# Which engine copies the turned attention probabilities out of PSUM: two of three on VectorE and one on ScalarE, in place of one and two

## The chip, the cores and the metric

The kernel runs on one core of a Trainium2 chip. The metric is the time of one execution on the device in microseconds; less is better. Of the core's engines five are spoken of here: TensorE (PE in the profile, with its weight loads as PEld), VectorE (DVE), ScalarE (ACT), GpSimd (POOL) and SyncE (SP), which only issues transfers in this kernel.

## The reference, cut to what matters

Two transformer blocks over 256 tokens of width 1024, in float32. The first block has eight heads of dilated attention and eight heads of dense causal attention, and a dense feed-forward net. The second block has two layers: sixteen heads of compressed, selected and windowed attention (called NSA below), then sixteen heads of block attention (MoBA); each layer has a mixture of 32 experts and a gated embedding. At 256 tokens every one of these attentions is a softmax over at most 256 keys:

```python
logits = einsum('bqhd,bkhd->bhqk', qi, k) * scale      # plus a bias, or a mask
p = softmax(where(mask, logits, -inf), axis=-1)
out = einsum('bhqk,bkhd->bqhd', p, v)
```

The product with `v` contracts over keys, so the probabilities, which come out with queries on the partitions, must be turned to have keys on the partitions.

## The kernel before

All attention runs through `class Pair` (L612): two heads side by side. `scores()` (L618) has PE make the scores of both heads (eight matmuls, L622, tile `sps`); DVE adds the bias and takes the row maximum (L629, four instructions); ACT takes the exponential and the row sum (L631, four instructions); DVE takes the reciprocal of the sums (L633) and, in NSA, multiplies in a gate (L635); POOL scales the probabilities (L638, four instructions). `turn()` (L640) has PE transpose the three 128x128 blocks of each head into a PSUM bank (L645, tile `ptp`) and then copies 384 columns of the bank into SBUF as `PT` (L648): one copy a head, two a pair, put on ACT or DVE by a counter `nev` that runs over the whole kernel. `pv()` (L652) has PE multiply `PT` with the values (L654, L656, tile `ops`). In NSA four more matmuls follow every second pair (L1827). `Out.put` (L688) then takes the result of a head pair out of PSUM in two parts (ACT at L691, DVE at L692).

`attend()` (L664) sets the order: step i issues the scores of pair i, the turn of pair i-2 and the product of pair i-3. So a copy is used by PE one step after it is issued. There are 8 pairs in the first block, 16 in NSA and 8 in MoBA: 32 pairs, 64 copies.

The instructions of PE and SP run in the order of the program text, which is written by hand (`manual_schedule(engines={ENG.PE, ENG.SP})`, L265). The order of the others, DVE, ACT and POOL, is set by a planner when the program is built. P and PT come from one pool of five buffers (`sq2`, L270, `PB = 5`), PSUM banks from one pool of eight (`bank`, L267).

`stream()` (L435) puts other work between the steps of attention. In the first block and in NSA this is the rest of a projection and what hangs on it (`second()`, L1481 and L1884), and from some step on the first halves of the output projection (`OutProj.part`, L699; its matmuls are L541 to L543, and each weight tile is split into two parts by ACT, L536, and DVE, L537, or POOL). In NSA `second()` also normalises the second half of the queries: ACT squares (L603), DVE sums (L604), DVE works out the reciprocal root in small steps (L457 to L479), DVE scales one half of the tokens and POOL the other (L1571), and PE transposes the result (L730, tile `htp`) ahead of the scores of the pairs that need it.

After attention the arena that holds the weights gets room again and the transfers of the following stage run on.

Of the kernel before, what the change touches and what calls it, by code (L numbers as in the profile page):

```python
# [251 lines left out]
def block_kernel(ctx, tc, I, out):  # L252
    nc = tc.nc
    mm = nc.tensor.matmul
    V, A, G = nc.vector, nc.scalar, nc.gpsimd
# [11 lines left out]
    def bank(name="bank"):  # L267
        return psum.tile([128, 512], F32, tag="bank", name=name)

    def sq2(name="sq"):  # L270
        return pr.tile([128, 512], F32, tag="sq", name=name)
# [12 lines left out]
    def drop(*keys):  # L284
        for k in keys:
            arena.drop(k)
        W.pump()
# [318 lines left out]
    nev = [0]  # L606
# [5 lines left out]
    class Pair:  # L612
# [27 lines left out]
        def turn(self):  # L640
            self.pt = []
            for p in self.p:
                b = bank("ptp")
                for i in range(3):
                    nc.tensor.transpose(b[:, i * 128:(i + 1) * 128], p[:, i * 128:(i + 1) * 128], ident)  # L645
                pt = sq2("PT")
                nev[0] += 1
                (A.copy if nev[0] % 3 else V.tensor_copy)(pt[:, 0:384], b[:, 0:384])  # L648
                self.pt.append(pt)
            drop(f"P{id(self)}")  # L650

# [216 lines left out]
    def moe(l, router, rs):  # L868
# [195 lines left out]
        def overflow(T):  # L1064
# [4 lines left out]
            with tc.If(n > 0):  # L1069
                with tc.For_i(0, n, 1):  # L1070
# [44 lines left out]
                    for k in range(8):  # L1115
                        mm(b[:, 0:256], R.xe[:, k], gu[:, :, k * 128:(k + 1) * 128], start=k == 0, stop=k == 7)
                    hidden(R)
                    turn(R)
                    for c in range(2):
                        b = R.bank(f"y{c}")  # L1120
# [8 lines left out]
        for q in range(8):  # L1129
# [34 lines left out]
            for _ in range(0 if q else 3):  # L1164
                next(fill, None)
            turn(T)
            for _ in range(9 if q else 1):
                next(fill, None)
# [876 lines left out]
```

## Time and profile before

| | before |
|---|---|
| time, median of 3 runs | 880.39 us (879.73 to 885.22) |
| profiled execution, its own time | 883.1 us |
| its span, first to last instruction | 881.3 us |
| PE busy | 829.3 us (94%) |
| DVE busy | 512.2 us (58%) |
| ACT busy | 453.0 us (51%) |
| POOL busy | 225.0 us (26%) |
| mean clock granted to PE | 0.971 of full |

The profiled execution is one run, taken by itself; its time stands 0.3% above the median. A busy time is the time an engine spent in instructions. The ends of matmuls are modelled, so short waits of PE between matmuls do not show as idle time; they show on PEld or as a longer distance between starts. [...] Attention takes three stretches of the span: about 96 to 125 us, 401 to 473 us and 694 to 729 us.

### The profile page before, as it was taken

The numbers are of one execution on the slowest core, as the hardware profiler recorded it, in microseconds if no ns is written. First come the engines' busy times: TensorE is split into PE (matmuls) and PEld (weight loads), VectorE is DVE, ScalarE is ACT, GpSimd is POOL, SyncE is SP. The second block draws the span as 40 slices with busy tenths as digits, with TensorE's granted clock in tenths as the row PEclk, the third lists the DMA queues.
The fourth block names the chain that finished last, engine by engine and source line by source line (L and its number), as shares of the span: only waits on it lengthen the run. The fifth ranks groups of instructions, "written<-read, shape, count | busy, mean of one in ns | idle before, by whom it ended". The sixth has DMA issues, their size and how long they took to land. (4 is left out here: it accounts for less than half of the span.)

```text
span 881.3 us, 15729 instructions
## 1 busy us (share of the span) xinstructions
PE 829.3 (94%) x5660; PEld 647.4 (73%) x5660; DVE 512.2 (58%) x1479; ACT 453.0 (51%) x1106; POOL 225.0 (26%) x293
## 2 busy tenths in 40 slices
PE   8997999999999999999899999965899899999997
PEld 5995878999999988686667666635587778666656
DVE  5669656755454567678664544321688765543355
ACT  6675875544444456267675133420666774232463
POOL 2225542322222234214453200000122355000011
PEclk9998999999999999999799999995999899999999
DMA  9990429655556542446015699999463515799961
GB/s 307 385 375 31 146 81 399 237 191 171 198 179 188 182 144 96 161 141 237 1 50 197 254 378 406 408 397 379 157 207 129 208 66 193 293 384 406 408 262 49
DMA packets 85137, 200.05 MB, mean 227 GB/s; under 512 B 5776, under 2 KB 27584, under 8 KB 85056
## 3 DMA queue, kind: packets, MB, share of 16 engines
q1 hardware_dynamic: 82704, 195.61, 61.1%
q10 hardware_dynamic: 2352, 3.40, 1.1%
q8 instruction: 46, 0.75, 0.3%
q14 instruction: 35, 0.29, 0.1%
HBM read 197.93 MB, written 1.06 MB: 226 GB/s over the span
## 5 line engine op out<-in xcount | busy, mean ns | idle before, releaser
L537 DVE TENSOR_TENSOR s<-a,s 128x512 fp32r<-128x512 f32 (+3 forms) x281 | 189.5, 685 | 121.7 <-ACT s L536 87.0
L536 ACT CAST s<-a 128x512 fp32r<-128x512 f32 (+3 forms) x294 | 172.6, 600 | 169.8 <-PE pj L543 71.7
L541 PE MATMUL pj<-s,a 128*128 128x512 f32 (+3 forms) x456 | 176.1, 386 | 4.6 <-ACT a L518 3.0
L542 PE MATMUL pj<-s,a 128*128 128x512 f32 (+3 forms) x456 | 170.5, 374 | 5.9 <-DVE s L537 5.8
L543 PE MATMUL pj<-s,a 128*128 128x512 f32 (+3 forms) x456 | 170.4, 374 | 1.3 <-DVE a L519 1.2
L537 POOL TENSOR_TENSOR s<-a,s 128x512 fp32r<-128x512 f32 (+3 forms) x71 | 90.1, 1269 | 304.6 <-ACT s L536 246.6
L541 PEld LDWEIGHTS pj<-s,a 128*128 128x128 f32 x456 | 86.4, 190 | 24.1 <-issue 5.6
L534 POOL TENSOR_SCALAR s<-a 128x512 fp32r<-128x512 f32 (+3 forms) x58 | 40.3, 696 | 242.3 <-PE pj L543 113.9
L542 PEld LDWEIGHTS pj<-s,a 128*128 128x128 f32 x456 | 86.7, 190 | 20.1 <-DVE s L537 7.8
L543 PEld LDWEIGHTS pj<-s,a 128*128 128x128 f32 x456 | 86.6, 190 | 18.2 <-DVE a L519 3.6
L1517 PE MATMUL f<-a,s 128*128 128x256 f32 x256 | 72.6, 284 | 0.0
L1519 PE MATMUL f<-a,s 128*128 128x256 f32 x256 | 72.4, 283 | 0.0
L1518 PE MATMUL f<-a,s 128*128 128x256 f32 x256 | 72.4, 283 | 0.0
L1027 PE MATMUL gu<-a,xe 128*32 128x256 f32 x1024 | 58.7, 380 | 0.7 <-DVE xe L1002 0.7
L1027 PEld LDWEIGHTS gu<-a,xe 128*32 128x32 f32 x1024 | 32.5, 110 | 28.4 <-issue 4.9
L541 PE MATMUL acc<-s,a 128*128 128x512 f32 x128 | 50.1, 391 | 0.0
L542 PE MATMUL acc<-s,a 128*128 128x512 f32 x128 | 49.9, 390 | 0.0
L543 PE MATMUL acc<-s,a 128*128 128x512 f32 x128 | 49.8, 389 | 0.0
L1518 PEld LDWEIGHTS f<-a,s 128*128 128x128 f32 x256 | 49.1, 192 | 0.2
L1517 PEld LDWEIGHTS f<-a,s 128*128 128x128 f32 x256 | 49.1, 192 | 0.2
L1519 PEld LDWEIGHTS f<-a,s 128*128 128x128 f32 x256 | 49.1, 192 | 0.0
L638 POOL TENSOR_SCALAR P<-P,nd 128x128 f32<-128x128 f32 x64 | 30.2, 483 | 58.7 <-DVE nd L633 18.1
(365 smaller groups left out, 1426.1 us busy)
## 6 DMA issues: line engine op xcount, KB each, us to landing
a<-in_w_ff_dram SPq DMA_DIRECT2D x32, 1024.0 KB, 5.5
a<-in_moe_w_gate_dram SPq DMA_DIRECT2D x64, 512.0 KB, 6.8
a<-in_moe_w_up_dram SPq DMA_DIRECT2D x64, 512.0 KB, 7.5
a<-in_moe_w_down_dram SPq DMA_DIRECT2D x32, 1024.0 KB, 8.8
a<-in_a_w_in_dram SPq DMA_DIRECT2D x10, 1024.0 KB, 5.1
a<-in_ple_w_gate_dram SPq DMA_DIRECT2D x8, 1024.0 KB, 15.6
a<-in_w_in_dram SPq DMA_DIRECT2D x6, 1024.0 KB, 14.4
a<-in_w_o_dram SPq DMA_DIRECT2D x4, 1024.0 KB, 13.8
```

What stands on the lines that cost most here:

```text
L534: G.tensor_scalar(hi, wv, 1.0, 0.0, OP.mult, OP.add)
L536: A.copy(hi, wv)
L537: (G if nsplit[0] % 5 == 2 else V).tensor_tensor(lo, wv, hi.bitcast(F32), OP.subtract)
L541: mm(ps, xh, hi, start=st, stop=False)
L542: mm(ps, xh, lo, start=False, stop=False)
L543: mm(ps, xl, hi, start=False, stop=sp)
L638: G.tensor_scalar(p[:, o0:o0 + n], p[:, o0:o0 + n], rc[:, t, i:i + 1], 1.0, OP.mult, OP.mult)
L1027: mm(b[32 * e:32 * e + 32, 0:256], T.xe[:, k, 32 * e:32 * e + 32], w, start=k == 0, stop=k == 7)
L1517: mm(o, hi[:, fs], xt[0][:, k], start=st, stop=False)
L1518: mm(o, hi[:, fs], xt[1][:, k], start=False, stop=False)
L1519: mm(o, lo[:, fs], xt[0][:, k], start=False, stop=sp)
```

## The change

The counter stays, and the two choices are exchanged. Of 64 copies, 43 were on ACT and 21 (each third) on DVE; now 43 are on DVE and 21 (each third) on ACT. Source, destination, size and everything else stay.

```diff
                 pt = sq2("PT")
                 nev[0] += 1
-                (A.copy if nev[0] % 3 else V.tensor_copy)(pt[:, 0:384], b[:, 0:384])
+                (V.tensor_copy if nev[0] % 3 else A.copy)(pt[:, 0:384], b[:, 0:384])
                 self.pt.append(pt)
```

## Rows read from the trace of the kernel before

**Rows 1.** The page's busy time by engine, share of the span, instructions

```profile
PE 829.3 (94%) x5660; PEld 647.4 (73%) x5660; DVE 512.2 (58%) x1479; ACT 453.0 (51%) x1106; POOL 225.0 (26%) x293
```

**Rows 2.** Busy time of each engine in four stretches, then PEclk, DMA share, GB/s

```profile
113.00:118.00 5.00, 5.00 (x44) 3.22 (x42) 3.51 (x22) 4.93 (x22) 2.91 (x8) 1.00 0.05 20
...
710.00:715.00 5.00, 4.88 (x43) 3.10 (x39) 4.20 (x23) 5.00 (x22) 2.64 (x7) 1.00 0.01 3
...
416.80:424.50 7.70, 6.38 (x56) 3.92 (x52) 7.57 (x40) 7.63 (x31) 5.38 (x12) 1.00 0.09 36
...
445.00:455.00 10.00, 10.00 (x71) 7.07 (x72) 6.94 (x34) 7.33 (x27) 5.80 (x12) 1.00 0.01 2
```

**Rows 3.** Timeline of PE: start, length, what; attention steps in three stretches

```profile
109.82 0.93 PE L622 MATMUL sps<-a 64*128 64x128 f32 x8
...
117.74 0.93 PE L622 MATMUL sps<-a 64*128 64x128 f32 x8
...
702.65 0.93 PE L622 MATMUL sps<-a,a 64*128 64x128 f32 x8
...
713.50 0.93 PE L622 MATMUL sps<-a,a 64*128 64x128 f32 x8
...
413.95 0.93 PE L622 MATMUL sps<-a,a 64*128 64x128 f32 x8
...
417.45 0.93 PE L622 MATMUL sps<-a,a 64*128 64x128 f32 x8
...
419.91 0.93 PE L622 MATMUL sps<-a,a 64*128 64x128 f32 x8
...
443.51 0.60 PE L1827 MATMUL ops<-a,a 128*64 128x256 f32 x4
444.04 0.93 PE L622 MATMUL sps<-a,a 64*128 64x128 f32 x8
```

**Rows 4.** The copies, line L648, by engine: shortest, median, longest in ns

```profile
L648 ACT COPY PT<-ptp x43: 451/472/498, 108.0 to 724.1; 128x384 f32<-128x384 f32 x43
...
L648 DVE COPY PT<-ptp x21: 543/553/559, 109.3 to 723.8; 128x384 f32<-128x384 f32 x21
```

**Rows 5.** Timelines of ACT and DVE: a copy and the next start

```profile
111.07 0.49 ACT L648 COPY PT<-ptp 128x384 f32<-128x384 f32 x1
111.43 0.40 ACT L691 CAST a<-ops 128x256 fp32r<-128x256 f32 x1
...
122.93 0.54 DVE L648 COPY PT<-ptp 128x384 f32<-128x384 f32 x1
123.40 0.41 DVE L692 TENSOR_TENSOR a<-ops,a 128x256 fp32r<-128x256 f32 x1
```

**Rows 6.** PE's waits at tile PT (us, times), and two weight loads of the timeline

```profile
  ACT PT L648: 2.8, 9
...
712.71 0.13 PEld L654 LDWEIGHTS ops<-PT,a 128*64 128x64 f32 x1 [0.57 <-ACT PT L648]
...
419.11 0.20 PEld L654 LDWEIGHTS ops<-PT,a 128*64 128x64 f32 x4 [0.17 <-issue]
```

**Rows 7.** Timelines of NSA's query chain: ACT, DVE, POOL, PE

```profile
416.07 0.68 ACT L603 ACTIVATE sq<-pj,r 128x512 f32<-128x512 f32 x1
...
415.04 0.29 DVE L629 CUSTOM_DVE_ANT_0 a<-sps,cst 128x128 f32<-128x128 f32 x1 [0.77 <-PE sps L622]
...
416.79 0.69 DVE L604 TENSOR_REDUCE stage<-sq 128x8 f32<-128x512 f32 x1
...
422.61 0.84 DVE L1571 TENSOR_TENSOR a<-a,stage 128x512 f32<-128x512 f32 x1
...
424.63 1.03 POOL L1571 TENSOR_TENSOR a<-a,stage 128x512 f32<-128x512 f32 x1
...
425.72 0.55 PE L730 MATMUL htp<-ident_r,a 128*128 128x128 f32 x3 [1.82 <-POOL a L1571]
```

**Rows 8.** Busy time of each engine, then PEclk, DMA share, GB/s, 428 to 437 us

```profile
428.00:437.00 9.00, 9.00 (x46) 7.24 (x46) 4.01 (x19) 3.56 (x13) 1.62 (x4) 0.50 0.01 3
```

## The prediction

> **What bounds the kernel now.** I began with the busy time by engine [rows 1]: PE 94%, DVE 58%, ACT 51%. Over the span neither of the two engines between which copies move is near its limit, so I read next the stretches in which the copies run. The busy time by stretch [rows 2] shows another picture: in the middle of the first block's attention ACT is busy 4.93 of 5.00 us and DVE 3.51; in MoBA ACT 5.00 and DVE 4.20; in the first half of NSA both are full, ACT 7.63 and DVE 7.57 of 7.70; in the second half, where the output projection fills in, ACT has 7.33 and DVE 6.94 of 10.00. So the change takes work from a full engine in two stretches, gives it to a full one in a third, and moves it between two loose ones in the last.
>
> A full engine is not yet the one that sets the time. PE's order is written by hand, so I read PE's timeline as a clock: the distance between the scores of one pair and of the next, where nothing is filled in between [rows 3]. The step from 417.45 to 419.91 in NSA is 2.46 us; inside it PE shows only short gaps at changes of operation, such as the 0.17 that is put to issue [rows 6]. I take 2.46 us as what PE itself needs for a pair. The first block takes 117.74 - 109.82 = 7.92 us for three steps, 0.54 above three times 2.46. MoBA takes 713.50 - 702.65 = 10.85 for four, 1.01 above. NSA's step from 413.95 to 417.45 takes 3.50, and it holds four more matmuls; such four take 444.04 - 443.51 = 0.53 a little later, so 0.51 is left over. ACT and PE are thus nearly level: ACT's full load makes PE late by 0.54 + 1.01 + 0.51 = 2.1 us in all, not more.
>
> What PE waited for says how much of that is the copies. At tile PT, PE stood idle until an ACT copy for 2.8 us, 9 times [rows 6]. One of these is the 0.57 us at 712.71. The gap of 0.17 is there without a late copy too, so 2.8 - 9 x 0.17 = 1.3 us is real waiting.
>
> **The change part by part.** *Engine time.* 22 copies net leave ACT for DVE (43 to 21). One takes 472 ns on ACT and 553 on DVE in the median [rows 4], but the next instruction starts earlier: 0.36 us after a copy on ACT (111.07 to 111.43) and 0.47 on DVE (122.93 to 123.40) [rows 5]. ACT loses 22 x 0.36 = 7.9 us and DVE gains 22 x 0.47 = 10.3 us. Neither is a change of the time by itself.
>
> *What speaks against it.* Out of PSUM the copy is 81 ns longer on DVE [rows 4]. [...]
>
> *The relief.* Per pair ACT has 4/3 copies now and 2/3 after, so 0.67 x 0.36 = 0.24 us less; DVE has 0.67 x 0.47 = 0.31 more. In the first block and MoBA, DVE has room: 0.31 us on a step of 2.46 against 1.49 us idle in 5.00, and 0.80 in 5.00 in MoBA, two steps each [rows 2]. PE can win the 1.3 us it really waited for copies, as an upper bound the 2.1 us above its own pace, and nothing as the lower. I take 1.3, since a copy is used one step after it is made and 0.24 us a pair is more than the lateness per pair (2.1 us over eight steps, 0.26, of which the copies are 0.16).
>
> *The query chain in NSA.* Here DVE is full and its work ends in something PE waits for: ACT squares (416.07), DVE sums (416.79), small steps to the scale at 422.61, POOL's half at 424.63, and PE's transposes at 425.72 after 1.82 us of idle time [rows 7]. Ahead of 422.61 stand nine copies of this stretch, numbers 17 to 25 of the counter. Now DVE has 18, 21 and 24; after, it has the six others. That is 3 x 0.47 = 1.4 us more on DVE in front of the chain's end. Against it, DVE has 0.77 us idle at 415.04 [rows 7], and ACT has 3 x 0.36 = 1.1 us less, which can bring the squares forward. Bounds: 0 and +1.4 us; I take the middle, +0.7. What is late next is POOL's half, then PE's transposes, and with them every step behind, since PE runs in order.
>
> *The second half of NSA and the last steps of MoBA.* PE is busy all the 10.00 us of 445 to 455 [rows 2], with the output projection's matmuls between the steps, and ACT and DVE have 2.7 and 3.1 us to spare: 0.31 us a step of about 4 us is covered. If that cover went, it would cost at most 0.31 us a step.
>
> *The copy's own length.* 81 ns later for PE on each moved copy, 0 because it is used a step later, 1.8 us if PE waited for each of the 22.
>
> *What else could move.* The copy on DVE took 543 to 559 ns whatever POOL was doing beside it [rows 4], so I give nothing for DVE and POOL getting in each other's way. No transfer is added or moved, and none of a queue's instructions is passed. A copy at the head of DVE's queue that waits for PE or for a buffer holds the maxima behind it, and ACT's exponentials wait for these; that is within the bounds above as long as the planner puts copies behind the maxima, as it does now. The planner may set DVE, ACT and POOL in another order; the rows do not price that.
>
> *The sum.* -1.3 + 0.7 = -0.6 us. It carries through to the end, either way: in the second half of NSA the transfers are at 2 GB/s [rows 2], because they wait for the arena's room, so a later or earlier end of attention moves them along. Against the profiled execution, 883.1 us, that is 882.5; it stands 2.7 us above the median of the runs, and from the median, 880.4 - 0.6 = 879.8 us.
>
> **The rivals.** *Hidden anyway.* PE's pace of 2.46 us holds, the waits for late ACT copies come back as waits for late DVE copies or for maxima behind them, and the query chain takes its 0 from the lower bound: 880.4 us. For it: ACT and PE are almost level already. Against it: 0.57 us at one place is plainly ACT's queue.
>
> *DVE becomes the bound in NSA (the slower side).* The query chain takes the whole 1.4 us, and the relief is nothing because DVE's copies are as late: 880.4 + 1.4 = 881.8 us. It decides once DVE's lateness at 422.61 is over 1.3 us. For it: 7.57 of 7.70 us busy [rows 2]. Against it: ACT ahead of it gets 1.1 us freer. That every moved copy keeps PE 81 ns longer [rows 4] is worth 880.4 + 1.8 = 882.2 us and counts here.
>
> *ACT was the bound after all.* If the first block and MoBA shorten by all that ACT loses there: 16 pairs at 0.24 us, 3.8 us, so 876.6 us. For it: 5.00 of 5.00 busy. Against it: the steps of 2.46 us without a wait, beyond which PE cannot go.
>
> [...]
>
> **How the numbers follow.** Chances: the forecast, 879.8, with its own range 878.5 to 881.0 (the two bounds of relief and chain), 0.45; hidden anyway 0.2; DVE the bound 0.18; ACT the bound 0.1; a low clock 0.04; the planner's order somewhere beyond these, either way, 0.03. For the range I go from the case that ACT was the bound, 876.6, to beyond the slower rival with a microsecond for runs that differ (the three of before differ by 0.66 and 4.8 us), 883.8. What is left out is less than 2 in 10. One per cent, which is about what a measurement of this kernel can tell from no change, is 8.8 us: none of the cases reaches it. Faster by over 1% 0.02, within 1% 0.95, slower by over 1% 0.03.
>
> **What would show it.** Right: DVE has 43 copies of about 553 ns and ACT 21 of 472; ACT's busy time falls by some 8 to 10 us and DVE's rises by 10 to 12; in the first block and MoBA, steps of 2.46 us with ACT no longer full; PE's waits at PT for ACT well under 2.8 us; in NSA the DVE scaling later than its place against the first scores of the stage by 0 to 1.4 us. Wrong: steps over 2.7 us where nothing is filled in, weight loads that wait for DVE's PT, a new stretch at half clock, or a gap ahead of PE's query transposes of over 4 us.

## The result, and the profile after

The changed kernel takes 875.28 us (median of 4 runs, 874.14 to 876.18) against 880.37 us for the kernel before, timed beside it (4 runs, 879.73 to 885.22): a ratio of 0.9924, 95% interval 0.9895 to 0.9954. Timed again later beside others it took 875.08 us (10 runs) against 880.77 (27 runs), ratio 0.9938, 0.9918 to 0.9957. So it is 0.6 to 0.8% faster, within the one per cent that the prediction called no change, but 4.5 us under the predicted 879.8 us and 1.3 us under the low end of the range, 876.6.

The runs of one kernel spread here by several microseconds: the kernel before by 877.62 to 886.9 us in those 27, the changed one by 873.13 to 876.91. That spread turns out to be the subject.

The profiled execution of the changed kernel took 876.2 us with a span of 874.4; that of the kernel before, 883.1 and 881.3. Busy time by engine, to be set against [rows 1], and the copies by engine, against [rows 4]:

```profile
PE 824.1 (94%) x5660; PEld 643.5 (74%) x5660; DVE 520.4 (60%) x1501; ACT 446.3 (51%) x1084; POOL 226.0 (26%) x293
...
L648 DVE COPY PT<-ptp x43: 542/551/559, 106.6 to 718.6; 128x384 f32<-128x384 f32 x43
L648 ACT COPY PT<-ptp x21: 452/462/483, 110.6 to 717.8; 128x384 f32<-128x384 f32 x21
```

The copies went where the diff sends them, 43 to DVE and 21 to ACT. DVE gained 8.2 us and ACT lost 6.7. PE lost 5.2 us of busy time with the same 5660 matmuls: it did the same work faster.

What PE and its weight loads waited for at tile PT (us, times), against [rows 6]:

```profile
  ACT PT L648: 0.7, 2
  DVE PT L648: 0.5, 2
```

From 2.8 us, 9 times, to 1.2 us, 4 times. Now PE's timeline (start, length, what), against [rows 3]: the first block, then the same four steps of MoBA.

```profile
110.01 0.93 PE L622 MATMUL sps<-a 64*128 64x128 f32 x8
...
117.40 0.93 PE L622 MATMUL sps<-a 64*128 64x128 f32 x8
...
696.39 0.93 PE L622 MATMUL sps<-a,a 64*128 64x128 f32 x8
...
699.30 0.93 PE L622 MATMUL sps<-a,a 64*128 64x128 f32 x8
...
701.76 0.93 PE L622 MATMUL sps<-a,a 64*128 64x128 f32 x8
...
704.84 0.93 PE L622 MATMUL sps<-a,a 64*128 64x128 f32 x8
...
707.30 0.93 PE L622 MATMUL sps<-a,a 64*128 64x128 f32 x8
```

Three steps of the first block take 7.39 us, three times 2.46; before they took 7.92. MoBA's four take 10.91; before, 10.85. So the first block gave its 0.53 us and MoBA nothing. Lined up instruction by instruction (PE's order is the same in both), PE is 0.4 us ahead of the kernel before at the end of the first block, 2.0 at the start of NSA, 6.3 at its end, and 6.2 at the end of the kernel. NSA holds most of it, and this is the place, on PE:

```profile
411.95 0.93 PE L622 MATMUL sps<-a,a 64*128 64x128 f32 x8
...
414.96 0.93 PE L622 MATMUL sps<-a,a 64*128 64x128 f32 x8
...
417.84 0.93 PE L622 MATMUL sps<-a,a 64*128 64x128 f32 x8
...
422.51 0.66 PE L730 MATMUL htp<-ident_r,a 128*128 128x128 f32 x4 [0.91 <-DVE a L1571]
423.10 0.93 PE L622 MATMUL sps<-a,a 64*128 64x128 f32 x8
...
433.70 0.44 PE L1807 MATMUL ctp<-ident_r,a 128*128 128x128 f32 x2 [1.37 <-DVE a L1802]
...
434.87 0.93 PE L622 MATMUL sps<-a,a 64*128 64x128 f32 x8
```

Ahead of the query transposes (L730) PE waited before for DVE's half of the query, 0.72 us, and then for POOL's, 1.82 us [rows 7]. The first of the two waits, in the kernel before:

```profile
423.59 0.30 PE L730 MATMUL htp<-ident_r,a 128*128 128x128 f32 x1 [0.72 <-DVE a L1571]
```

In the changed kernel there is one wait of 0.91. POOL's half now starts at 420.87 and DVE's at 420.99:

```profile
420.87 1.04 POOL L1571 TENSOR_TENSOR a<-a,stage 128x512 f32<-128x512 f32 x1 [1.52 <-DVE nd L635]
...
420.99 1.47 DVE L1571 TENSOR_TENSOR a<-a,stage 128x512 f32<-128x512 f32 x1
```

Counted from the scores ahead of it (419.91 before [rows 3], 417.84 after), DVE's half starts 0.45 us later than before, POOL's 1.69 us earlier. The planner had put POOL's half behind the four L638 of a pair; in the changed kernel it stands ahead of them.

Side by side the two engines took longer here. DVE's half takes 1.47 us beside POOL's half, 0.63 more than the 0.84 of before [rows 7], and PE's wait of 0.91 ends with it. In the kernel before it was POOL that took long: two of its L638, beside DVE's L1571 and L537, took 1.77 us where the two ahead of them took 0.82, and POOL's half stood behind these:

```profile
422.88 1.77 POOL L638 TENSOR_SCALAR a<-a,nd 128x128 f32<-128x128 f32 x2
```

The prediction gave nothing for DVE and POOL getting in each other's way; it had looked at the copies alone, and these do keep their length (542 to 559 ns, above).

PE's clock over 11 us behind the gap (busy time of each engine, then the granted clock, the share of DMA, GB/s), first the kernel before, then the changed one:

```profile
427.00:438.00 11.00, 11.00 (x60) 8.82 (x60) 5.37 (x27) 5.07 (x19) 2.11 (x6) 0.53 0.01 2
```

```profile
427.00:438.00 11.00, 9.63 (x88) 6.20 (x90) 9.75 (x48) 6.92 (x28) 5.39 (x12) 1.00 0.01 2
```

Before, PE was granted 0.53 of its full clock over these 11 us, and 0.50 in each of the nine from 428 to 437 [rows 8], and got 60 matmuls done; after, 1.00 throughout and 88. Half clock, below, is a granted clock of 0.50; a loss of clock is one minus the granted clock, summed over stretches of 1 us: 5.1 us here before, nothing after.

Against that, the profile of before has another stretch at half clock, 355 to 360 us (1.7 us lost), that the changed kernel lacks, though the gap in front is the same (1.84 and 1.85 us, for POOL's L1609). This part of the code isn't touched. So a stretch at half clock can come and go by itself, and the experiments had to say which of the gain is the change's.

### The profile page after: what moved, and what is told of

The parts are those of the page before. It is cut to its first block, busy times and chain, and to the rows that moved or that the text cites. A ratio compares the mean times of both kernels' runs of the same rounds, so it can differ in the third digit from the quotient of the medians.

```text
span 874.4 us, 15706 instructions
## 1 busy us (share of the span) xinstructions
PE 824.1 (94%) x5660; PEld 643.5 (74%) x5660; DVE 520.4 (60%) x1501; ACT 446.3 (51%) x1084; POOL 226.0 (26%) x293
## 5 line engine op out<-in xcount | busy, mean ns | idle before, releaser
L537 DVE TENSOR_TENSOR s<-a,s 128x512 fp32r<-128x512 f32 (+3 forms) x281 | 189.6, 685 | 127.0 <-ACT s L536 92.8
L537 POOL TENSOR_TENSOR s<-a,s 128x512 fp32r<-128x512 f32 (+3 forms) x71 | 90.4, 1273 | 302.8 <-ACT s L536 247.1
L543 PEld LDWEIGHTS pj<-s,a 128*128 128x128 f32 x456 | 86.6, 190 | 18.2 <-DVE a L519 3.6
L638 POOL TENSOR_SCALAR P<-P,nd 128x128 f32<-128x128 f32 x64 | 30.9, 495 | 50.8 <-DVE nd L633 18.3
```

The costliest lines, as they stand in the source:

```text
L537: (G if nsplit[0] % 5 == 2 else V).tensor_tensor(lo, wv, hi.bitcast(F32), OP.subtract)
L543: mm(ps, xl, hi, start=False, stop=sp)
L638: G.tensor_scalar(p[:, o0:o0 + n], p[:, o0:o0 + n], rc[:, t, i:i + 1], 1.0, OP.mult, OP.mult)
```

## The experiments

**One stretch of the kernel at a time.** The counter `nev` is 1 to 16 in the first block, 17 to 48 in NSA and 49 to 64 in MoBA.

```diff
# nsa_only, and nsa_again (the same kernel once more)
-                (A.copy if nev[0] % 3 else V.tensor_copy)(pt[:, 0:384], b[:, 0:384])
+                (V.tensor_copy if (nev[0] % 3 > 0) == (17 <= nev[0] <= 48) else A.copy)(pt[:, 0:384], b[:, 0:384])
# first_moba
+                (A.copy if (nev[0] % 3 > 0) == (17 <= nev[0] <= 48) else V.tensor_copy)(pt[:, 0:384], b[:, 0:384])
# first_only
+                (A.copy if (nev[0] % 3 > 0) == (nev[0] > 16) else V.tensor_copy)(pt[:, 0:384], b[:, 0:384])
```

> The change in NSA's 32 copies alone (numbers 17 to 48 of the counter); the first block and MoBA keep two of three copies on ScalarE. Theory: most of the gain sits in NSA, where the gap ahead of the query transposes L730 became shorter (2.9 us of PE idle between 422.8 and 425.7 before, about 1.4 after) and the stretch at half clock behind it is gone. Then this kernel is 4 to 5 us faster than before, and its trace has the clock at 1.00 behind L730. Rival: ScalarE was the bound in all three attentions, 0.24 us a pair; then this kernel gains about half of 5 us, 2.5 us or less, and the half clock stays.

> The kernel before with the new split in NSA alone, looked at a second time. Theory (the shorter gap ahead of NSA's query transposes takes the half clock behind it away): no granted clock under 0.97 between 420 and 440 us; the gap is one wait of 0.9 us; median 3.5 to 5 us under the kernel before (876 to 877.3), which leaves about half a microsecond to the first block and nothing to MoBA. Rival (draws): a half-clock stretch in NSA, median less than 2.5 us under the kernel before.

> The change in the first block's and MoBA's 32 copies alone; NSA keeps two of three copies on ScalarE. Theory: 0.5 us in the first block (steps of 2.46 us in place of 7.92 us for three) and 0.0 in MoBA, so 0.5 us faster, and the half clock at about 428 to 437 us stays. Rival (ScalarE the bound everywhere): 2.5 us or more faster.

> The kernel before with the new split of the copies in the first attention block alone (the first 16 copies); NSA and MoBA keep the old one. Theory: the first block's steps lose 0.5 us of waits at the copies, nothing else moves, and PE still stands 0.7 and 1.8 us ahead of NSA's query transposes, so the half clock behind them stays: median 0.5 us under the kernel before, at most 1.5 us under it (879.3 to 880.5). Still open, and to be seen here: the half clock at 355 to 360 us stood in three of four executions with the old split in this block and in none of six with the new one. If the split of this block decides it, although it ends 235 us earlier, the stretch is absent and the median is 1.7 to 2.5 us under the kernel before; if it is a draw, either may come.

| kernel | median us (runs) | lowest to highest | ratio to before, 95% |
| --- | --- | --- | --- |
| nsa_only | 876.05 (6) | 874.01 to 877.04 | 0.9953 (0.9932 to 0.9974) |
| nsa_again | 875.50 (12) | 874.04 to 878.50 | 0.9952 (0.9937 to 0.9968) |
| first_moba | 876.59 (6) | 875.52 to 880.66 | 0.9968 (0.9941 to 0.9995) |
| first_only | 877.90 (12) | 874.85 to 882.37 | 0.9977 (0.9952 to 1.0002) |

NSA alone gives about 4.2 us by the ratios, most of the whole. The other two missed their expectations: 0.5 us was expected of each, and first_moba is 2.8 us faster by the ratio (4.2 by the medians) and first_only 2.0 (2.4), so that the parts sum to more than the whole. First_moba reached the number of its rival, ScalarE as the bound everywhere, but its profile doesn't bear the rival out: in the profiles of first_only and of first_moba the first block is 0.54 us shorter, as in the changed kernel, and in first_moba MoBA's four steps take 10.89 us. What the times show is two groups: six of first_only's twelve lie at 874.85 to 876.81 us with a granted clock of 0.977 to 0.982, six at 879.0 to 882.37 with 0.969 to 0.975; of first_moba's six, four lie at 875.52 to 876.81 with 0.979 and two at 880.6 with 0.972. Why so many of these executions keep the clock, with NSA's copies as before, isn't shown. MoBA is settled by executions without half clock there: the four steps take 10.85 us with the old split (first_only, 694.78 to 705.63) and 10.89 with the new one (after_again, 693.33 to 704.22). Its relief is nothing.

The surprise is first_only in NSA, where it has the old split and both waits, and in this execution no half clock; here are PE and the clock from 420 to 440 us:

```profile
418.89 0.93 PE L622 MATMUL sps<-a,a 64*128 64x128 f32 x8
...
422.57 0.30 PE L730 MATMUL htp<-ident_r,a 128*128 128x128 f32 x1 [0.72 <-DVE a L1571]
424.69 0.55 PE L730 MATMUL htp<-ident_r,a 128*128 128x128 f32 x3 [1.82 <-POOL a L1571]
425.17 0.93 PE L622 MATMUL sps<-a,a 64*128 64x128 f32 x8
...
435.53 0.93 PE L622 MATMUL sps<-a,a 64*128 64x128 f32 x8
...
420.00:440.00 20.00, 17.46 (x154) 12.29 (x152) 15.97 (x79) 15.18 (x56) 10.76 (x24) 1.00 0.00 1
```

And the same steps in nsa_again, with the new split:

```profile
418.75 0.93 PE L622 MATMUL sps<-a,a 64*128 64x128 f32 x8
...
423.42 0.66 PE L730 MATMUL htp<-ident_r,a 128*128 128x128 f32 x4 [0.91 <-DVE a L1571]
...
434.24 0.44 PE L1807 MATMUL ctp<-ident_r,a 128*128 128x128 f32 x2 [1.01 <-DVE a L1802]
435.41 0.93 PE L622 MATMUL sps<-a,a 64*128 64x128 f32 x8
...
420.00:440.00 20.00, 17.91 (x155) 12.37 (x153) 16.82 (x86) 14.27 (x54) 10.69 (x23) 1.00 0.01 2
```

From the first to the last of these scores the old split takes 16.64 us and the new one 16.66; the changed kernel, above, takes 434.87 - 417.84 = 17.03. At full clock NSA gains nothing. PE passes the query transposes 1.0 us sooner and then waits 1.0 to 1.4 us for L1802, the last step of the comparison scores on the fuller DVE. The kernel before took 21.23 us for the same steps, from 419.91 [rows 3] to

```profile
441.14 0.93 PE L622 MATMUL sps<-a,a 64*128 64x128 f32 x8
```

With the same two waits as first_only, its difference of 4.6 us is its half clock.

**The kernels themselves again,** unchanged.

> The kernel before, unchanged, looked at a second time, to learn which half-clock stretches belong to it and which were the draw of one execution. Theory (the 2.1 us that PE stands ahead of NSA's query transposes bring the half clock behind them): a half-clock stretch begins between 424 and 430 us again, 2 to 5 us long in loss, while the one at 355 to 360 may be absent. Rival (every stretch behind a gap is a draw, NSA's like the others): no granted clock under 0.97 between 420 and 440 us. Both expect a median of 880 to 881 us.

> The changed kernel, unchanged, looked at a second time and timed beside the three others. Theory: no half clock between 415 and 440 us, as in its first execution; the loss of clock over the whole span about 18 to 19 us, against 21 to 22 of the kernel before; median 875 to 876 us. Rival (a draw): a half-clock stretch in NSA this time, and a median within 2 us of the kernel before, 878.5 to 881.

Before_again took 879.90 us (12 runs), after_again 875.08 (10). The kernel before has half clock in NSA again, shorter (1.7 us lost); after_again has none. The window of before_again:

```profile
426.00:430.00 4.00, 4.00 (x24) 3.61 (x21) 1.76 (x9) 2.71 (x10) 0.66 (x2) 0.57 0.00 0
```

**The gap put back.** The copies stay as in the changed kernel; the second half of the queries is normalised three rests later (a rest is a turn of the filler work that issues nothing), so that the planner has POOL's half behind the L638 again.

```diff
+        yield from rest(3)
         q_norm(1, qn1)
-        yield from rest(8)
+        yield from rest(5)
```

> The changed kernel with the normalising of the second half of NSA's queries held back: three of the eight rests that stood behind it stand ahead of it, so that GpSimd turns to its half of the query only behind one more pair's four L638 than in the kernel before. The copies stay as in the changed kernel. PE should stand 2 to 3 us longer ahead of its query transposes than in the changed kernel, so about as long as in the kernel before or 1 us longer. Theory (the gap brings the half clock): a half-clock stretch is back behind it, from about 425 us, with 3 to 5 us of loss; the loss over the span 21 us or more; median 879 to 881 us. Rival (the split of the copies itself keeps the clock up, or the stretch is a draw): only the gap is paid, no half clock in NSA; median 877 to 878 us.

It took 881.55 us (12 runs, 878.81 to 886.77), 6.5 us more than after_again beside it. PE and the clock:

```profile
423.37 0.33 PE L730 MATMUL htp<-ident_r,a 128*128 128x128 f32 x1 [2.70 <-DVE a L1571]
425.52 0.90 PE L730 MATMUL htp<-ident_r,a 128*128 128x128 f32 x3 [1.82 <-POOL a L1571]
...
423.00:424.00 1.00, 0.33 (x1) 0.14 (x1) 0.32 (x1) 0.00 (x0) 1.00 (x3) 0.80 0.00 0
...
423.00:431.00 8.00, 5.81 (x30) 4.64 (x30) 1.85 (x11) 3.24 (x11) 2.55 (x5) 0.57 0.00 1
```

The half clock is back with 3.4 us lost. With the new split of the copies unchanged, it is the longer gap that brings it, as the theory had it, and the split by itself doesn't keep the clock up. In the timed runs the loss over the span was 21.5 us in the mean against 18.0 for after_again, so of the 6.5 us some 3.5 are clock (an estimate) and the rest would be waiting. The waits came out 2 us longer than those of the kernel before, 4.5 us in all against 2.5, and the half clock began between them, behind the first of 2.70 us. So it isn't the old gap that was put back but a longer one.

**The gap shortened another way,** by choosing the engine of the second query's halves: both on VectorE with the old split (before_qv and before_qv_again), both on GpSimd with the new one (after_qg).

```diff
-    def q_norm(c, qn):
+    def q_norm(c, qn, e=None):
...
-            qk_norm(qn[:, t], ov[:, t], 8, G if t else V)
+            qk_norm(qn[:, t], ov[:, t], 8, e or (G if t else V))
...
-        q_norm(1, qn1)
+        q_norm(1, qn1, V)        # after_qg, on the changed kernel: G
```

> The kernel before with one edit: in NSA both halves of the second query group are scaled on VectorE (L1571); GpSimd's half, which came 2 us after VectorE's, is gone. No copy is moved. Theory: the gap ahead of L730 decides over the clock behind it. VectorE ends its second half some 0.8 us after the first, so PE waits until about 424.5 in place of 425.7; if that is short enough the half clock goes and the time falls by 3 to 5 us without any copy moved. If the gap is still too long, 1 us faster and the half clock stays. Rival (ScalarE's relief is the cause): no change within 0.5 us, since ScalarE keeps all its copies.

> The kernel before with both halves of NSA's second query normalised on VectorE and the old split of the copies, looked at a second time, since its ten times (878.9 in the median) and its one execution (no half clock in NSA) did not fit one another. Theory by the gap alone: PE's waits ahead of the query transposes are 0.7 and 0.2 us, so no half clock between 420 and 440 us, and the median 3 to 4.5 us under the kernel before. Rival (two waits of 0.9 us in all are still long enough in some executions, or the old split leaves other gaps behind them): a half-clock stretch between 420 and 440 us in this execution, and a median 1 to 2.5 us under the kernel before.

> The kernel after with one edit: in NSA both halves of the second query group are scaled on GpSimd, one after the other (L1571). All copies stay as in the kernel after. Theory: PE waits about 1 us longer ahead of L730, the gap grows to some 2.5 us, the half clock comes back, and 3 to 5 us of the gain are lost, far more than the 1 us of waiting. Rival: ScalarE's relief is the cause; then at most 1 us is lost and the clock stays at 1.00.

After_qg: 876.76 us (10 runs, ratio 0.9948, 0.9933 to 0.9963), waits of 0.36 and 0.67 us ahead of the transposes, no half clock in NSA. The expectation had the gap grow to 2.5 us and bring the half clock back; it came out at 1.0 in two parts, so this run doesn't test the theory as it was meant to. By the ratios it is 0.9 us slower than after_again (0.9948 against 0.9938), as its rival had it. Before_qv and before_qv_again: 878.88 and 878.53 us (10 and 12 runs; ratios 0.9986, 0.9971 to 1.0002, and 0.9980, 0.9963 to 0.9997), 1.2 to 1.8 us under the kernel before by the ratios and not the 3 to 4.5 that the theory of the gap alone asked for. In before_qv_again PE has another wait, ahead of the matmuls of NSA's comparison scores (L1779):

```profile
423.31 0.55 PE L730 MATMUL htp<-ident_r,a 128*128 128x128 f32 x3 [0.21 <-DVE a L1571]
...
427.60 1.09 PE L1779 MATMUL csp<-stage,a 128*128 128x32 f32 x8 [0.83 <-ACT a L731]
...
428.00:432.00 4.00, 4.00 (x25) 2.59 (x25) 2.15 (x7) 0.89 (x2) 1.20 (x3) 0.57 0.03 6
```

POOL's wait is gone, but ACT is late with the turned query, L731, PE waits for it, and half clock follows this time; in before_qv the same wait of 0.83 us stands and half clock doesn't follow. The rival named in the expectation holds. But this wait isn't the old split's own. After_qg has it too, with no half clock behind it:

```profile
427.28 1.08 PE L1779 MATMUL csp<-stage,a 128*128 128x32 f32 x8 [0.88 <-ACT a L731]
```

So with nearly the same waits in NSA the old split lost 20.7 and 20.5 us of clock over the span in the timed runs and the new one 18.2. What the new split adds to a shorter gap isn't shown.

**Half clock in NSA, all fourteen profiles.** Waits are those ahead of the query transposes, and those behind them at L1779 and L1807 (for L1802).

| kernels | copies in NSA | waits, us | clock lost at 420 to 440, us |
| --- | --- | --- | --- |
| before, before_again, first_moba, first_only, before_gap_cmp | old | 0.7 + 1.8 | 5.1, 1.7, 1.7, 0, 5.1 |
| after_late | new | 2.7 + 1.8, then 1.1 at L1807 | 3.4 |
| before_qv, before_qv_again | old | 0.7 + 0.2, then 0.8 at L1779 | 0, 1.7 |
| after_qg | new | 0.4 + 0.7, then 0.9 at L1779, 1.1 at L1807 | 0 |
| after, after_again, nsa_only, nsa_again, gap_cmp | new | 0.9, then 1.0 to 1.4 at L1807 | 0, 0, 0, 0, 0 |

With the long pair of waits five of six executions pay, 2.8 us in the mean; with one wait of 0.9 us there none of five does. The timed runs say the same of the whole span: one minus the granted clock, times the span, is 20.9 to 21.8 us in the mean for the three groups of 23 to 35 runs of the kernel before and for before_again, 18.8 and 18.0 for the changed one, 17.9 and 18.9 with NSA's split alone, 21.1 for first_only, 20.4 for first_moba and 21.5 for after_late. Beside the kernel before, the short gap loses 2.0 us less in nsa_again, 3.3 in after_again and 3.9 in nsa_only.

**The same lesson at another gap.** Ahead of L1692, some 50 us before NSA's attention, PE waits 1.85 us for additions on GpSimd (L1609). The last two of the eight go to VectorE, which idles there (2.02 us ahead of its L537 at 354.29 in the kernel before), in the changed kernel (gap_cmp) and in the kernel before (before_gap_cmp).

```diff
-                G.tensor_tensor(blkT[:, w, :, 2 * (f % 2) + i, 0:15], view, pp, OP.add)
+                (V if f == 3 else G).tensor_tensor(blkT[:, w, :, 2 * (f % 2) + i, 0:15], view, pp, OP.add)
```

> The changed kernel with the last two of the eight L1609 additions on VectorE, which idles 2.0 us there, in place of GpSimd: on GpSimd the last one stands behind an L537 and an L534 of a weight tile, and PE waits 1.85 us for it ahead of L1692. The same lesson on another gap: theory says the wait of 1.85 us falls under 0.5 us, which is 1.4 to 1.8 us off the span in any case, and that the half clock at 355 to 360 us, which showed in two of six executions, goes too: median 873 to 874 us. Rival: the transposes' copies on VectorE fall behind the two additions and the wait stays, 875 to 876 us.

> The kernel before with the last two of the eight L1609 additions on VectorE, and the copies as they were: the wait of 1.85 us ahead of L1692 falls to about 0.5 us, and no half clock follows at 355 to 360 us, where it stood in three of four executions with the old split. Theory: 1.3 us of the wait and about 1.3 us of clock in the mean, so a median 2 to 3.3 us under the kernel before (877.5 to 878.8), with NSA's half clock as before. Rival (what that place gives comes back later, at the next gap): 0 to 1.3 us under it.

PE's L1692 in the changed kernel, and in gap_cmp:

```profile
354.64 7.12 PE L1692 MATMUL cmph<-a,a 128*64 128x256 f32 x62 [1.85 <-POOL a L1609]
```

```profile
352.81 7.09 PE L1692 MATMUL cmph<-a,a 128*64 128x256 f32 x62 [0.53 <-POOL s L537]
```

Gap_cmp took 872.22 us (6 runs, 871.79 to 874.1), 2.9 us under after_again beside it and 8.6 under the kernel before (ratio 0.9907, 0.9877 to 0.9937): the fastest here. The wait is 1.3 us shorter, by direct reading; 1.5 us less clock was lost over the span (16.5 against 18.0), though after_again's profile had no half clock at 355, so where that came from isn't shown. Before_gap_cmp took 878.38 us (12 runs, ratio 0.9979, 0.9964 to 0.9994), 1.9 us under the kernel before: just short of the theory's 2 to 3.3 and above the rival's 1.3, with NSA's half clock in full (5.1 us lost).

## Why the prediction was wrong, by its own steps

**The relief at the copies, -1.3 us: right in kind, too large.** The 0.54 us of the first block came in full; I had all of it in the upper bound only. The 1.01 of MoBA didn't come at all, and of NSA's 0.51 next to nothing: the step of 3.50 us became 3.01, but the next, 2.46, became 2.88. I had put MoBA's excess down to ACT's full load. With ACT at 4.68 of 5.00 us there after the change, two of the four steps are still 2.9 and 3.1 us long: in one PE's loads wait for POOL's L638 (0.32 us), in the other for one of the copies that stayed on ACT (0.42):

```profile
698.13 0.20 PEld L645 LDWEIGHTS ptp<-ident_r,a 128*128 128x128 f32 x2 [0.32 <-POOL a L638]
...
704.04 0.13 PEld L654 LDWEIGHTS ops<-PT,a 128*64 128x64 f32 x1 [0.42 <-ACT PT L648]
```

Why the steps of 2.46 us beside them were spared is what I should have asked. Two slips in the working changed nothing: the 0.24 us a pair is less than the lateness of 0.26 it is set against, not more, and the bounds of relief and chain give 878.3 to 881.8 us, not 878.5 to 881.0.

**The query chain, +0.7 us (0 to 1.4): about right, by another path.** Of the three copies more that I put on DVE ahead of its half, the planner put two there (five against three). The half started 0.45 us later and, beside POOL's, ran 0.63 longer: 1.08 us late by its end, inside the bounds. But PE had been waiting for POOL's half, and this came 1.69 us earlier because the planner moved it ahead of a pair's L638. I wrote that the rows do not price the planner's order and gave it 0.03 of the chance. What DVE owed then fell due at L1802. Net, at full clock, the stage costs 17.03 - 16.64 = 0.4 us more in the changed kernel (0.0 in nsa_again).

So the sum of the engines' work, which I gave as -0.6, is -0.54 + 0 + 0.4, about -0.1 us at full clock.

**The clock, priced at nothing: the step that failed.** I had the half clock of 428 to 437 in the rows [rows 8], gave a low clock 0.04 of the chance, and put nothing for the stretch that was there into the sum. That was wrong. I held the gap itself at its length, as if what PE waited for could only come later, and took the stretch behind it as fixed. The gap shrank from two waits of 0.72 and 1.82 us to one of 0.91, and the stretch went: about 2.8 us in the mean of the executions with the long gap, 2.0 to 3.9 us by the loss of clock in the timed runs. The faster rival, 876.6, reached nearly to the result, but for a reason that wasn't the cause: ACT wasn't the bound in any stretch beyond 0.54 us.

**From one profile to the median.** I set the sum off against the profiled execution and moved it to the median. That execution, 2.7 us above the median, held one of the two longest NSA stretches seen (5.1 us) and the one at 355. Its 6.9 us of difference to the execution after are 0.5 us of first block, 1.7 of the draw at 355, 4.2 in NSA and half a microsecond elsewhere.

**What stays open.** The medians differ by 5.1 to 5.7 us. The first block's 0.5 is shown, 3 us of clock follow from the loss, and the other steps sum to +0.4, so some 2 to 2.6 us have no place in the profiles; the intervals of the ratios, 1.7 to 2.6 us to either side, could hold that, and no run tells. Why the same gap is followed by 0, 1.7, 3.4 or 5.1 us of loss isn't shown either. At 355 us half clock stood in four of twelve executions with the long wait there (1.7 us lost in each of before, before_again, before_qv and first_only), three of them with the old split in the first block and one with the new: a draw, as far as the runs go. A third place of this kind is 688 to 701 us, ahead of MoBA's steps, behind a wait of 1.5 us at PE's L501: half clock stood there in before, after and before_qv_again (3.4 us lost in each) and in after_late (1.7), and not in before_again, first_only, nsa_again, after_again, gap_cmp and before_gap_cmp. From the start of this L501 (691.94) to the scores at 702.65 [rows 3] the kernel before takes 10.71 us; first_only, nsa_again, after_again and before_gap_cmp take 8.59 or 8.60 for the same, 2.1 us less. That the gap decides is shown with the new split alone, by a gap longer than the old one. With the old one a shorter gap gave 1.2 to 1.8 us, and half of first_only's executions were fast with the long gap, so a part of the split's own in keeping the clock up isn't ruled out.

Of the signs listed, the copies' counts, the waits of ACT's at PT and the first block's steps came out as the right ones. ACT's and DVE's busy times moved less than said (6.7 us for 8 to 10, 8.2 for 10 to 12). Two of the wrong ones came: MoBA's steps of 2.9 and 3.1 us, and weight loads that wait for DVE's PT (0.5 us). "A gap ahead of the query transposes of over 4 us" was on the list of wrong ones, and a shorter one on neither.

## What to carry to other kernels

Where a profile shows half clock behind a gap on PE, price the gap together with its stretch, and in both directions: ask of each edit whether the gap gets shorter, not only whether a new one comes. A copy moved between engines also reorders the queues that a planner fills, so follow the last instruction that PE waits for at each long gap, here POOL's, and ask what it stands behind. And when a stretch comes and goes from one execution to the next, one pair of profiles doesn't measure a change: compare the steps at full clock instruction by instruction, and the clock over many runs.

## What the runs showed of the hardware

Waits of 0.7 and 1.8 us with one matmul of 0.30 us between them were followed by a granted clock of 0.50 in four of five executions (before, before_again, first_moba, before_gap_cmp). It began 1.1 to 1.7 us after the end of the second wait in the three of them whose clock was read microsecond by microsecond (all but first_moba), and the loss was 1.7 us in two of the four and 5.1 in two; behind the longer waits of after_late it was 3.4. Single waits of 1.37, 1.36 and 1.01 us at L1807 (after, after_again, nsa_again) were followed by none. Between 420 and 440 us half clock stood in the fourteen profiles only behind a wait of PE, the shortest of them the 0.83 us of before_qv_again; the same 0.83 us in before_qv and the two waits of 0.72 and 1.82 us in first_only passed without it.

The spread of the times goes with it. The kernels with one wait of 0.9 us spread by 2.3 to 4.5 us from lowest to highest (gap_cmp, nsa_only, after_again, nsa_again; 6 to 12 runs), those with the long pair by 5.1 to 8.0 (first_moba, before_again, first_only, after_late; 6 to 12 runs) and the kernel before by 9.0 to 9.7 in its groups of 23 to 35. Before_gap_cmp, 2.8 us with the long pair, is the exception.

DVE and POOL took longer where both worked at L1571 and L638: DVE's half of the query took 1.47 us in the changed kernel, where POOL's half ran beside it, and 0.84 in the kernel before; there two L638 of POOL took 1.77 us beside DVE's L1571 and L537, and the two ahead of them 0.82. The copies from PSUM stayed at 542 to 559 ns on DVE (before, after).
